# Second projection of an MLP: every third 256-row block of the weight computed by seven half-block products

## The chip, the core and the metric

The kernel runs on one core of a Trainium2 chip. Its time is the device time of one execution in microseconds; the median of three runs is given. Five engines work side by side: TensorE (PE in the profile, with its weight loads apart as PEld) multiplies matrices, VectorE (DVE) and ScalarE (ACT) do elementwise work, GpSimd (POOL) does next to nothing here, and SyncE (SP) issues the transfers from device memory. TensorE writes to eight banks of PSUM, 128 partitions by 512 fp32 columns each; everything else lies in SBUF.

## The reference

A decoder layer on 256 tokens of width 2048: a mixing part with three branches, then the MLP, and a last norm. The change touches the MLP alone, and in it the product with `w_mlp_out`.

```python
h = rmsnorm(x, norm1_g); proj = h @ w_in             # 2048 columns in, three branches, gates
...
x = x + merged @ w_out
h2 = rmsnorm(x, norm2_g)
x = x + jnp.square(jax.nn.relu(h2 @ w_mlp_in)) @ w_mlp_out   # (256,2048)@(2048,8192), then (256,8192)@(8192,2048)
return rmsnorm(x, final_g)
```

All is fp32. To keep its precision, each fp32 operand is split into a high part (rounded to the format fp32r) and a low part (the rest), and a product is three fp32r matmuls: high by high, low by high, high by low.

## The kernel before

**Units.** All weights come in units of 512 KB: 256 rows by 512 columns, held as a tile [128, 2, 512]. `plan` lists the stages of the program, and each stage's units have running numbers, in the order in which TensorE uses them. `dma_to` issues the transfer of a unit on SyncE's queue into a `raw` buffer; there are 4 of them (NRAW), used in turn. `conv_to` makes the two parts: ScalarE copies `raw` to `hi`, which rounds it, and VectorE subtracts, `lo = raw - hi`. `hi` and `lo` have 4 buffers each, in turn. A `raw` buffer is free for the next transfer when the subtraction has read it, a `hi` or `lo` buffer when the last matmul has read it.

**Order.** The order on every engine is that of the program text, and no engine overtakes itself. `begin_unit(u, 3)` stands ahead of the matmuls of unit u: it issues the transfer of unit u+5, then the conversion of unit u+3, then whatever was put off until now by `later` (the reading of finished sums from PSUM, above all). So in VectorE's queue the conversion of unit u+3 stands before the work on sums that comes due at unit u.

**The MLP.** The 8192 hidden columns are done in 4 quarters q. In each, 8 stages `m1` (256 hidden columns each, four units, 16 matmuls a unit, half of them 512 columns wide and half 256) produce the activations, held as `ff` tiles in two parts; then 4 stages `m2` (`run_N`) each multiply them with 512 of the output columns: 8 units, and for each unit 12 matmuls of 512 columns, for two token halves, two 128-row tiles and three products. The sums of a stage lie in one double bank out of two (`two_banks`, pool `ps_mm`, 2 buffers); its end is read one unit later, by two operations of VectorE that add it to the running `x2`, while TensorE works on in the other double bank. Four more single banks (`side`) are not used by these stages. The last stage (`run_last`) orders its matmuls by output, and a norm follows it.

## Time and profile before

| | us |
|---|---|
| median of 3 runs (1542.29 to 1542.65) | 1542.41 |
| the profiled execution, its own time | 1541.8 |
| its span, first to last instruction | 1540.0 |
| TensorE busy | 1529.7 |
| VectorE busy | 1097.5 |
| ScalarE busy | 762.7 |

The profiled execution's time is 1.8 us more than its span, and 0.6 us less than the median. A row of the timeline reads: start in us, duration in us, engine, line, operation, output<-inputs, and in brackets the idle time of the engine before it and what ended it. A row of a group reads: line, engine, operation, names, shapes, count | busy us, mean ns of one | idle time before it and what ended it. A row of the windows reads: stretch in us: its length, then busy time (and count of instructions) of PE, PEld, DVE, ACT and POOL, TensorE's granted clock as a share of full speed, the busy share of the transfer engines, and GB/s. All of VectorE's instructions carry the line of a helper (L86), so they are told apart by names. Matmuls overlap: one of 512 columns is shown as 0.39 us long, and the next starts earlier than it ends.

### The profile page before, as it was taken

To read this page: it belongs to the slowest core of one execution; us is meant where nothing else is said; L and a number is where in the kernel's file an instruction comes from. 1 tells how busy PE (TensorE), PEld (TensorE's weight loads), DVE (VectorE), ACT (ScalarE), POOL (GpSimd) and SP (SyncE) were. 2 spreads that over 40 slices of the span, in tenths; PEclk is the share of its full clock that TensorE was granted. 3 is DMA by queue.
4 is the path that set the end of the run, shared out by engine and by line. 5 is a ranking of instruction groups with operands and counts; after the bars stand their busy time and mean duration, and the time that the engine had idled before them with its cause. 6 is when DMAs were issued, how large, how long until landed. Compare 5 with 4: busy or idle time off the path is not lost.

```text
span 1540.0 us, 20664 instructions
## 1 busy us (share of the span) xinstructions
PE 1529.7 (99%) x7948; PEld 1300.2 (84%) x7948; DVE 1097.5 (71%) x1456; ACT 762.7 (50%) x948; POOL 12.2 (1%) x21
## 2 busy tenths in 40 slices
PE   9999999999999999999999999999999999999997
PEld 9988888888888887898888888888888888888886
DVE  7886978989999999967655665456545655555554
ACT  7446678455555555564454443344433443344442
POOL 0000000000000000000000000000000000000000
PEclk9999999999999999999999999999999999999999
DMA  9654555555555566656666556555555555555653
GB/s 358 200 190 146 188 185 171 185 196 187 189 197 190 193 197 205 191 179 202 209 205 192 191 180 203 192 191 181 198 193 193 181 192 195 195 184 193 217 192 121
DMA packets 85506, 298.17 MB, mean 194 GB/s; under 512 B 9632, under 2 KB 10656, under 8 KB 85408
## 3 DMA queue, kind: packets, MB, share of 16 engines
q1 hardware_dynamic: 79200, 285.25, 55.9%
q10 hardware_dynamic: 6208, 11.61, 2.3%
q8 instruction: 62, 1.02, 0.3%
q14 instruction: 36, 0.29, 0.1%
HBM read 294.73 MB, written 2.10 MB: 193 GB/s over the span
## 4 chain that ended last, share of the span: by engine, by line
PE 96%; DVE 1%; ACT 1%; issue 1%; DMA 0%; POOL 0%; POOLq 0%; DVEq 0%; ACTq 0%
PE mm L288 20%; PE mm L350 20%; PE mm L351 19%; PE mm L353 19%; PE mm L292 10%; PE mm L320 2%; PE mm L319 2%; PE mm L327 1%; PE pb L642 1%; PE py L742 1%; DVE lo L86 0%; PE pwarm L468 0%; DMA raw<-in_w_m 0%; DVE x L86 0%; ACT hi L213 0%
## 5 line engine op out<-in xcount | busy, mean ns | idle before, releaser
L86 DVE TENSOR_TENSOR lo<-raw,hi 128x1024 fp32r<-128x1024 f32 (+1 forms) x537 | 653.7, 1221 | 377.9 <-ACT hi L213 366.1
L213 ACT CAST hi<-raw 128x1024 fp32r<-128x1024 f32 (+1 forms) x537 | 560.6, 1048 | 610.2 <-PE mm L351 377.6
L288 PE MATMUL mm<-xz,hi 128*128 128x512 f32 x1024 | 256.5, 392 | 0.0
L288 PEld LDWEIGHTS mm<-xz,hi 128*128 128x128 f32 x1024 | 184.4, 189 | 33.2
L350 PE MATMUL mm<-hi,xs 128*128 128x512 f32 x512 | 201.4, 393 | 0.0
L351 PE MATMUL mm<-hi,xs 128*128 128x512 f32 x512 | 199.6, 390 | 0.0
L351 PE MATMUL mm<-hi,ff 128*128 128x512 f32 x480 | 186.8, 389 | 0.0
L350 PE MATMUL mm<-hi,ff 128*128 128x512 f32 x480 | 186.8, 389 | 0.0
L292 PEld LDWEIGHTS mm<-xz,lo 128*128 128x128 f32 x1024 | 139.7, 190 | 10.0
L292 PE MATMUL mm<-xz,lo 128*128 128x256 f32 x1024 | 142.8, 282 | 0.0
L353 PE MATMUL mm<-lo,xs 128*128 128x512 f32 x512 | 136.9, 389 | 0.0
L353 PE MATMUL mm<-lo,ff 128*128 128x512 f32 x480 | 128.3, 389 | 0.0
L350 PEld LDWEIGHTS mm<-hi,xs 128*128 128x128 f32 x512 | 96.1, 188 | 23.5 <-issue 4.1
L353 PEld LDWEIGHTS mm<-lo,xs 128*128 128x128 f32 x512 | 96.1, 188 | 20.2
L351 PEld LDWEIGHTS mm<-hi,xs 128*128 128x128 f32 x512 | 96.2, 188 | 19.4
L353 PEld LDWEIGHTS mm<-lo,ff 128*128 128x128 f32 x480 | 90.1, 188 | 18.7
L351 PEld LDWEIGHTS mm<-hi,ff 128*128 128x128 f32 x480 | 90.1, 188 | 18.6
L350 PEld LDWEIGHTS mm<-hi,ff 128*128 128x128 f32 x480 | 90.1, 188 | 18.6
L288 PE MATMUL mm<-xs,hi 128*128 128x512 f32 x384 | 96.9, 394 | 0.0
L288 PEld LDWEIGHTS mm<-xs,hi 128*128 128x128 f32 x384 | 69.1, 189 | 13.6 <-issue 0.7
L86 DVE TENSOR_TENSOR rt<-bu,cs 128x1024 f32<-128x1024 f32 x64 | 76.6, 1220 | 0.3
L292 PEld LDWEIGHTS mm<-xs,lo 128*128 128x128 f32 x384 | 52.4, 190 | 3.8
(247 smaller groups left out, 1619.7 us busy)
## 6 DMA issues: line engine op xcount, KB each, us to landing
raw<-in_w_m SPq DMA_DIRECT2D x256, 512.0 KB, 4.3
raw<-in_w_in SPq DMA_DIRECT2D x143, 512.0 KB, 4.0
raw<-in_w_wide SPq DMA_DIRECT2D x48, 512.0 KB, 3.9
raw<-in_w_br SPq DMA_DIRECT2D x48, 512.0 KB, 4.2
raw<-in_w_out SPq DMA_DIRECT2D x32, 512.0 KB, 3.7
x<-in_x ACTq DMA_DIRECT2D x8, 512.0 KB, 6.1
raw<-in_w_glu SPq DMA_DIRECT2D x8, 512.0 KB, 4.6
gb<-in_b_gate ACTq DMA_DIRECT2D x12, 256.0 KB, 4.3
```

Source lines behind the costliest of these rows:

```text
L86: return fn(*a, **kw)
L213: S.copy(hi[:, k, :], raw[:, k, :])
L288: PE.matmul(pt[:, nb, :], lhsT=hi[:, k, nb * P:(nb + 1) * P], rhs=src.both(4 * i + k), start=4 * i + k == 0, stop=False)
L292: PE.matmul(pt[:, nb, T:], lhsT=lo[:, k, nb * P:(nb + 1) * P], rhs=src.hi(4 * i + k), start=False, stop=4 * i + k == last)
L319: PE.matmul(po, lhsT=wh, rhs=src.hi(kt), start=kt == 0 and nb % 2 == 0, stop=False)
L320: PE.matmul(po, lhsT=wh, rhs=src.lo(kt), start=False, stop=False)
L327: PE.matmul(po, lhsT=lo[:, k, nb * P:(nb + 1) * P], rhs=src.hi(kt), start=False, stop=kt == 2 * nk - 1 and nb % 2 == 1)
L350: PE.matmul(ps[tt], lhsT=xh, rhs=hi[:, k, :], start=kt == 0, stop=False)
L351: PE.matmul(ps[tt], lhsT=xl, rhs=hi[:, k, :], start=False, stop=False)
L353: PE.matmul(ps[tt], lhsT=xh, rhs=lo[:, k, :], start=False, stop=kt == 2 * nk - 1)
L642: PE.matmul(pbs[h][i][:, ri * T:(ri + 1) * T], lhsT=s5bs[h // 4][r, h % 4, ri * P:(ri + 1) * P], rhs=s5x[h // 4][r, h % 4, :], start=True, ...
L742: PE.matmul(py[h][32 * i:32 * i + 32, :T], lhsT=cks[h][:, ri, i, :], rhs=s[i // 2][:, ri, i % 2, :], start=ri == 0, stop=ri == 1, tile_pos ...
```

## The change

The division of the hidden columns and the products of `m2` change; the mixing part, `m1`'s matmuls and the last two stages stay as they are.

- The hidden columns are done in 3 parts of 12, 12 and 8 units (3072, 3072 and 2048 columns). Each `m2` pass of a part now makes 1024 output columns (half h), in all four PSUM banks of `ps_mm`: `top` for the first 128 tokens, `bot` for the others. Only the last two stages of the last part are as before.
- In such a pass, the units k = 0, 3, 6, 9 are done by `run_seven` in another way: a block of 2x2 half blocks (two token halves by two 128-row tiles by two 512-column halves) takes seven products of half blocks in place of eight, in the manner of Strassen and Winograd. Three of its operands on the token side, and three on the weight side, are sums and differences. The token side's four (`form`) are made once in `m1` by `sums`. The weight side's are made from the two transferred tiles in `conv_seven`: there are three conversion units, `a` (as it came), `c` (the difference `d`) and `e` (two more sums, and one half as it came, `b`), out of two transfers. `a`'s raw buffer is read until `e`'s sums, and `c`'s until `e`'s low part is done.
- Four of the seven products go to the four `side` banks, where they are shared by several outputs. They are read one unit after the last seven-product block (`ev_shared`); `top` and `bot` are read right behind their last products (`evac[1]`), at a place in the program that comes after the conversion of the next pass's first units. `m1`'s last group is read at once as well.
- `hi` and `lo` have 5 buffers each, and the pool of activations 32 in place of 34.

```diff
-NACT = 34
+NACT = 32
...
+PARTS = (12, 12, 8)
+FIRST = [sum(PARTS[:q]) for q in range(len(PARTS) + 1)]
+LAST = len(PARTS) - 1
+EVERY = 3
...
-    whi = ctx.enter_context(tc.tile_pool(name="whi", bufs=4))
-    wlo = ctx.enter_context(tc.tile_pool(name="wlo", bufs=4))
+    whi = ctx.enter_context(tc.tile_pool(name="whi", bufs=5))
+    wlo = ctx.enter_context(tc.tile_pool(name="wlo", bufs=5))
...
-    for q in range(4):
-        for i in range(0, 8, 2):
+    for q, nk in enumerate(PARTS):
+        for i in range(0, nk, 2):
+            g = FIRST[q] + i
             if (q, i) == (0, 0):
                 ab = [add_units(w_m1, 0, 0, 3), add_units(w_m1, 1, 0, 3)]
                 for j in range(2):
                     ab[j] += add_units(w_m1, j, 3, 4)
                 plan.append(("m1", (q, i), ab))
             else:
-                plan.append(("m1", (q, i), [add_units(w_m1, 8 * q + i + j, 0, 4) for j in range(2)]))
-        for i in range(4):
-            plan.append(("m2", (q, i), add_units(w_m2, i, 8 * q, 8 * q + 8)))
+                plan.append(("m1", (q, i), [add_units(w_m1, g + j, 0, 4) for j in range(2)]))
+        for h in range(2):
+            if (q, h) == (LAST, 1):
+                for c in (2, 3):
+                    plan.append(("m2", (q, c), add_units(w_m2, c, FIRST[q], FIRST[q + 1])))
+                continue
+            us = []
+            for k in range(nk):
+                ku = FIRST[q] + k
+                if k % EVERY == 0:
+                    n = len(units)
+                    units.extend((w_seven[h, ku // EVERY, 0], w_seven[h, ku // EVERY, 1], None))
+                    seven.update({n: "a", n + 1: "c", n + 2: "e"})
+                    us.append((n, n + 1, n + 2))
+                else:
+                    us.append([add_units(w_m2, 2 * h + c, ku, ku + 1)[0] for c in range(2)])
+            plan.append(("m2s", (q, h), us))
...
+            if units[u] is None:
+                raws.append(None)
+                continue
...
+    def split_unit(u, raw):
+        hi = whi.tile([P, 2, 512], F32R, tag="hi", name=f"hi{u}")
+        lo = wlo.tile([P, 2, 512], F32R, tag="lo", name=f"lo{u}")
+        S.copy(hi, raw)
+        V.tensor_sub(lo, raw, hi.bitcast(F32))
+        return hi, lo
+    def conv_seven(u, raw):
+        if seven[u] == "a":
+            part["a"] = raw
+            loaded[u] = split_unit(u, raw)
+        elif seven[u] == "c":
+            d = part["d"] = s5w.tile([P, 2, 512], F32, tag="T1", name=f"d{u}", bufs=1)
+            part["x"] = raw
+            V.tensor_sub(d, part["a"], raw[:, 0:1, :].to_broadcast([P, 2, 512]))
+            loaded[u] = split_unit(u, d)
+        else:
+            a, d, x = (part.pop(n) for n in "adx")
+            b = s5w.tile([P, 2, 512], F32R, tag="T2", name=f"b{u}", bufs=1)
+            S.copy(b[:, 0, :], x[:, 1, :])
+            V.tensor_sub(b[:, 1, :], x[:, 1, :], b[:, 0, :].bitcast(F32))
+            V.tensor_add(x[:, 0, :], d[:, 1, :], a[:, 0, :])
+            V.tensor_sub(x[:, 1, :], x[:, 1, :], x[:, 0, :])
+            loaded[u] = (*split_unit(u, x), b)
...
-                later(1, lambda pt=pt, evac=evac: evac(pt))
+                if at_once:
+                    evac(pt)
+                else:
+                    later(1, lambda pt=pt, evac=evac: evac(pt))
...
+    def run_seven(us, src, forms, evac):
+        top, bot = two_banks(f"top{us[0][0]}"), two_banks(f"bot{us[0][0]}")
+        bank = {(t, c): p[:, c, :] for t, p in enumerate((top, bot)) for c in range(2)}
+        for n in (1, 5, 7, 6):
+            bank[n] = side(f"p{n}_{us[0][0]}")
...
+        def half(kt, t):
+            return tuple(x[:, t * P:(t + 1) * P] for x in (src.hi(kt), src.lo(kt)))
+        def form(k, f):
+            return tuple(forms[k][:, f, e, :] for e in range(2))
+        def product(b, x, w):
+            mm(b, x[0], w[0])
+            mm(b, x[1], w[0])
+            mm(b, x[0], w[1])
+        def std(u, k, c, t, w):
+            for part in range(2):
+                for e in range(2):
+                    xh, xl = half(2 * k + e, t)
+                    if part == 0:
+                        mm((t, c), xh, w[0][:, e, :])
+                        mm((t, c), xl, w[0][:, e, :])
+                    else:
+                        mm((t, c), xh, w[1][:, e, :])
...
+        shared = max(k for k, u in enumerate(us) if len(u) == 3)
+        for k, u in enumerate(us):
+            if len(u) == 3:
+                a = begin_unit(u[0], 3)
+                product(1, half(2 * k, 0), [w[:, 0, :] for w in a])
+                end_unit()
+                d = begin_unit(u[1], 3)
+                product(5, form(k, 0), [w[:, 0, :] for w in d])
+                product(7, form(k, 2), [w[:, 1, :] for w in d])
+                product((0, 1), form(k, 3), [w[:, 1, :] for w in a])
+                end_unit()
+                hi, lo, b = begin_unit(u[2], 3)
+                product((0, 0), half(2 * k + 1, 0), (b[:, 0, :], b[:, 1, :]))
+                product(6, form(k, 1), (hi[:, 0, :], lo[:, 0, :]))
+                product((1, 0), half(2 * k + 1, 1), (hi[:, 1, :], lo[:, 1, :]))
+                if k == shared:
+                    later(1, lambda: evac[0](bank))
+                end_unit()
+            elif k < len(us) - 1:
+                for c in range(2):
+                    w = begin_unit(u[c], 3)
+                    for t in range(NT):
+                        std(u[c], k, c, t, w)
+                    end_unit()
+            else:
+                w0 = begin_unit(u[0], 3)
+                std(u[0], k, 0, 0, w0)
+                end_unit()
+                w1 = begin_unit(u[1], 3)
+                std(u[1], k, 1, 0, w1)
+                evac[1](0, top)
+                std(u[0], k, 0, 1, w0)
+                std(u[1], k, 1, 1, w1)
+                evac[1](1, bot)
+                end_unit()
...
+            def sums():
+                f = s5w.tile([P, 4, P], F32, tag="gb", name=f"sums{q}_{i}", bufs=1)
+                V.scalar_tensor_tensor(out=f[:, 0, :], in0=t[:, 0, P:], scalar=-1.0, in1=t[:, 1, P:],
+                                       op0=ALU.mult, op1=ALU.subtract)
+                V.scalar_tensor_tensor(out=f[:, 1, :], in0=f[:, 0, :], scalar=-1.0, in1=t[:, 0, :P],
+                                       op0=ALU.mult, op1=ALU.subtract)
+                V.tensor_sub(f[:, 2, :], t[:, 0, :P], t[:, 0, P:])
+                V.tensor_sub(f[:, 3, :], t[:, 1, :P], f[:, 1, :])
+                fs = forms[q][i] = a4([P, 4, 2, P], F32R, f"form{q}_{i}")
+                S.copy(fs[:, :, 0, :], f)
+                V.tensor_sub(fs[:, :, 1, :], f, fs[:, :, 0, :].bitcast(F32))
...
+                run_W([g], xs2, at_once=i0 + j == PARTS[q] - 1)
...
+    def do_m2s(q, h, us):
+        if q == LAST:
+            load_fg()
+        r = [a4([P, 2, 512], F32, f"m2r{q}{h}{t}") for t in range(NT)]
+        def ev_shared(bank):
+            p1, p12 = r[0][:, 0, :], r[0][:, 1, :]
+            p21, p22 = r[1][:, 0, :], r[1][:, 1, :]
+            S.copy(p1, bank[1])
+            S.copy(p12, bank[5])
+            V.tensor_add(p21, bank[6], p1)
+            V.tensor_add(p12, p12, p21)
+            V.tensor_add(p22, bank[7], p12)
+            V.tensor_add(p21, bank[7], p21)
+        def ev(t, ps):
+            V.tensor_add(r[t], ps, r[t])
+            for c in range(2):
+                later(1 + t, lambda c=c: add_m2(q, 2 * h + c, t, 0, 512, r[t][:, c, :]))
+        run_seven(us, ffs[q], forms[q], (ev_shared, ev))
...
+    b = a["w_m2"].reshape(2, 2, -1, P, 2, 512)[:, :, ::EVERY]
+    a["w_seven"] = np.stack([np.stack([b[:, r, :, :, 0], b[:, 1 - r, :, :, 1]], axis=3) for r in range(2)],
+                            axis=2)
```

**VectorE where one pass of the second projection ends and the next begins.** Names: `lo` is the low part of a weight unit, `mm` a double bank with finished sums, `x` the running output. Before, first part, from output columns 0 to 511 on to the next 512:

```order
L86 TENSOR_TENSOR lo_8405<-raw_8366,hi_8404 128x1024
L86 TENSOR_TENSOR lo_8423<-raw_8384,hi_8422 128x1024
L86 TENSOR_TENSOR lo_8441<-raw_8402,hi_8440 128x1024
L86 TENSOR_TENSOR lo_8460<-raw_8420,hi_8459 128x1024
L86 SCALAR_TENSOR_TENSOR x_0_6813<-mm_8304,rsq,x_0_6813 128x512 x2
L86 TENSOR_TENSOR lo_8480<-raw_8438,hi_8479 128x1024
L86 TENSOR_TENSOR lo_8498<-raw_8457,hi_8497 128x1024
L86 TENSOR_TENSOR lo_8516<-raw_8477,hi_8515 128x1024
```

The two sums are taken up in the middle of a row of conversions of plain units. In the change, from columns 0 to 1023 on to the next 1024; `m2r` is the tile into which the shared products and the sums are added, `p` a single bank, `d`, `b` and the second use of `raw` the weight sums of the next pass's first block:

```order
L91 TENSOR_TENSOR m2r_8728<-m2r_8728,m2r_8729 128x512
L91 TENSOR_TENSOR m2r_8729<-p_328_8734,m2r_8728 128x512
L91 TENSOR_TENSOR m2r_8729<-p_328_8734,m2r_8729 128x512
L91 TENSOR_TENSOR lo_9152<-raw_9112,hi_9151 128x1024
L91 TENSOR_TENSOR d_9169<-raw_9112,raw_9127 128x1024
L91 TENSOR_TENSOR lo_9172<-d_9169,hi_9171 128x1024
L91 TENSOR_TENSOR b_9183<-raw_9127,b_9183 128x512
L91 TENSOR_TENSOR raw_9127<-d_9169,raw_9112 128x512
L91 TENSOR_TENSOR raw_9127<-raw_9127 128x512
L91 TENSOR_TENSOR lo_9189<-raw_9127,hi_9188 128x1024
L91 TENSOR_TENSOR m2r_8728<-top_8730,m2r_8728 128x1024
L91 TENSOR_TENSOR m2r_8729<-bot_8731,m2r_8729 128x1024
```

The two operations on finished sums stood between conversions of plain units and nothing waited for them but the sums after next; now the two that read `top` and `bot` stand behind the three conversions a, c and e of the next pass.

**TensorE at the same place.** In the change, the end of the first pass (plain units of block 11) and the beginning of the second (products of block 0):

```order
L436 MATMUL bot_8731<-lo_9115,ff_11_8743 128x512 x2
L436 MATMUL bot_8731<-hi_9129,ff_11_8743 128x512 x4
L436 MATMUL bot_8731<-lo_9130,ff_11_8743 128x512 x2
L436 MATMUL p_356_9216<-hi_9151,ff_0_7732 128x512 x2
L436 MATMUL p_356_9216<-lo_9152,ff_0_7732 128x512
L436 MATMUL p_356_9217<-hi_9171,form_0_7765 128x512 x2
L436 MATMUL p_356_9217<-lo_9172,form_0_7765 128x512
L436 MATMUL p_356_9218<-hi_9171,form_0_7765 128x512 x2
L436 MATMUL p_356_9218<-lo_9172,form_0_7765 128x512
L436 MATMUL top_9214<-hi_9151,form_0_7765 128x512 x2
L436 MATMUL top_9214<-lo_9152,form_0_7765 128x512
```

Before, the next stage's first matmuls went to the other double bank. Now the third group of the new pass is written to `top` (`top_9214`), the same two banks as the `top_8730` just finished. The other passes end alike: after the second pass `m1`'s first group, and after the last part's pass the first plain stage, write to `top`'s banks at once.

**VectorE over one group of blocks, 3 to 5.** In the change (7 units for three blocks; the four rows at the end are the plain units), where before stood one `lo` a unit:

```order
L91 TENSOR_TENSOR lo_8798<-raw_8764,hi_8797 128x1024
L91 TENSOR_TENSOR d_8815<-raw_8764,raw_8779 128x1024
L91 TENSOR_TENSOR lo_8818<-d_8815,hi_8817 128x1024
L91 TENSOR_TENSOR b_8835<-raw_8779,b_8835 128x512
L91 TENSOR_TENSOR raw_8779<-d_8815,raw_8764 128x512
L91 TENSOR_TENSOR raw_8779<-raw_8779 128x512
L91 TENSOR_TENSOR lo_8841<-raw_8779,hi_8840 128x1024
L91 TENSOR_TENSOR lo_8859<-raw_8813,hi_8858 128x1024
L91 TENSOR_TENSOR lo_8868<-raw_8833,hi_8867 128x1024
L91 TENSOR_TENSOR lo_8883<-raw_8856,hi_8882 128x1024
L91 TENSOR_TENSOR lo_8898<-raw_8865,hi_8897 128x1024
```

The seven units of such a group have eleven operations of VectorE, where the six units of three plain blocks had six `lo`; each row here waits for a copy by ScalarE, except `d` and the two sums on `raw`.

## Rows read from the trace of the kernel before

**Rows 1.** The page: span, busy time by engine, the chain that ended last.

```profile
span 1540.0 us, 20664 instructions
...
PE 1529.7 (99%) x7948; PEld 1300.2 (84%) x7948; DVE 1097.5 (71%) x1456; ACT 762.7 (50%) x948; POOL 12.2 (1%) x21
...
PE 96%; DVE 1%; ACT 1%; issue 1%; DMA 0%; POOL 0%; POOLq 0%; DVEq 0%; ACTq 0%
```

**Rows 2.** Timeline, TensorE: one unit of the second projection and the next's start.

```profile
1101.89 0.39 PE L350 MATMUL mm<-hi,ff 128*128 128x512 f32 x1
...
1103.70 1.07 PE L353 MATMUL mm<-lo,ff 128*128 128x512 f32 x4
1104.61 0.39 PE L350 MATMUL mm<-hi,ff 128*128 128x512 f32 x1
```

**Rows 3.** Windows of one quarter's first projection, then of its second.

```profile
855.00:914.00 59.00, 59.00 (x341) 51.96 (x340) 36.35 (x37) 27.41 (x33) 0.00 (x0) 1.00 0.58 192
914.00:1004.00 90.00, 90.00 (x403) 74.72 (x403) 47.08 (x44) 35.89 (x36) 0.00 (x0) 1.00 0.58 193
```

**Rows 4.** Timeline of the second projection, ScalarE, then VectorE.

```profile
1112.06 1.05 ACT L213 CAST hi<-raw 128x1024 fp32r<-128x1024 f32 x1 [1.67 <-PE mm L351]
...
1113.14 1.23 DVE L86 TENSOR_TENSOR lo<-raw,hi 128x1024 fp32r<-128x1024 f32 x1 [1.49 <-ACT hi L213]
1114.28 1.40 DVE L86 SCALAR_TENSOR_TENSOR x<-mm,rsq,x 128x512 f32<-128x512 f32 x2
```

**Rows 5.** Groups by form, whole span, VectorE and ScalarE.

```profile
L86 DVE TENSOR_TENSOR lo<-raw,hi 128x1024 fp32r<-128x1024 f32 x535 | 652.3, 1223 | 377.3 <-ACT hi L213 365.5 <-PE mt L408 6.0 <-PE zt L408 4.5
L86 DVE TENSOR_TENSOR bu<-rt,rt 128x512 f32<-128x512 f32 x64 | 42.4, 693 | 0.4
L86 DVE TENSOR_TENSOR relu<-mm,relu 128x512 f32<-128x512 f32 x32 | 21.9, 684 | 0.0
L86 DVE SCALAR_TENSOR_TENSOR ck<-cu,cu 128x128 f32<-128x128 f32 x8 | 2.3, 285 | 0.0
...
L213 ACT CAST hi<-raw 128x1024 fp32r<-128x1024 f32 x535 | 559.3, 1050 | 609.7 <-PE mm L351 377.6 <-PE mm L288 119.9 <-issue 71.5
L399 ACT CAST ff<-relu 128x512 fp32r<-128x512 f32 x32 | 19.8, 619 | 60.9 <-DVE relu L86 60.9
L301 ACT COPY relu<-mm 128x512 f32<-128x512 f32 x32 | 18.7, 583 | 0.0
```

**Rows 6.** What SyncE's queue waited for, us in total, times, longest us.

```profile
SPq L194 <- DVE lo L86: 1231.2, 504, 7.8
```

**Rows 7.** Transfers of raw from issue to landing: 1098 to 1130, then 10 to 19 us.

```profile
DMA to landing us min/median/max: 3.7/4.3/4.5
...
DMA to landing us min/median/max: 6.1/6.5/7.5
```

**Rows 8.** The chain near the end, and the timeline of ScalarE there.

```profile
1510.77 4.32 DMA raw<-in_w_m
...
1515.10 1.05 ACT L213 CAST hi<-raw 128x1024 fp32r<-128x1024 f32 x1 [1.56 <-DMA raw<-in_w_m]
```

**Rows 9.** Windows of the end: TensorE's last matmuls, then none.

```profile
1531.00:1532.00 1.00, 0.69 (x6) 0.49 (x5) 0.27 (x1) 0.00 (x0) 0.00 (x0) 1.00 0.00 0
1532.00:1536.00 4.00, 0.00 (x0) 0.00 (x0) 2.47 (x7) 0.51 (x2) 0.55 (x1) 1.00 0.26 98
1536.00:1537.00 1.00, 0.00 (x0) 0.00 (x0) 0.00 (x0) 0.00 (x0) 0.00 (x0) 0.71 1.07 318
```

**Rows 10.** Timeline, TensorE: 256-column matmuls near the start, and a little later.

```profile
6.54 0.41 PE L320 MATMUL mm<-xs,hi 128*128 128x256 f32 x1
6.75 0.41 PE L319 MATMUL mm<-xs,hi 128*128 128x256 f32 x1
...
8.07 0.28 PE L320 MATMUL mm<-xs,hi 128*128 128x256 f32 x1
8.19 0.28 PE L319 MATMUL mm<-xs,hi 128*128 128x256 f32 x1
```

More of the change, by code (lines that the diff above doesn't have):

```diff
@@ L141, in side @@
         return ps_sd.tile([P, 512], F32, tag="sd", name=name)
-    units = []
+    units, seven = [], {}
     def add_units(src, g, k0, k1):
@@ L204, in conv_to @@
             raws[u] = None
+            if u in seven:
+                conv_seven(u, raw)
+                nconv[0] += 1
+                continue
             if u >= len(units) - 4:
@@ L358, in run_N, with mm @@
             end_unit()
+    def run_seven(us, src, forms, evac):
[3 more added lines that the diff above has]
+            bank[n] = side(f"p{n}_{us[0][0]}")
+        triples = sum(len(u) == 3 for u in us)
+        left = {b: 6 * (len(us) - triples) for b in bank if b not in (1, 5, 6, 7)}
+        for b in (1, 5, 6, 7, (0, 0), (0, 1), (1, 0)):
+            left[b] = left.get(b, 0) + 3 * triples
+        begun = set()
+        def mm(b, x, w):
+            left[b] -= 1
+            PE.matmul(bank[b], lhsT=x, rhs=w, start=b not in begun, stop=left[b] == 0)
+            begun.add(b)
+        def half(kt, t):
[50 more added lines that the diff above has]
+                end_unit()
+        assert not any(left.values())
@@ L1089, in square @@
                 split2(ffs[q], i, t)
+                if i % EVERY == 0:
+                    later(1, sums)
+            def sums():
[9 more added lines that the diff above has]
+                V.tensor_sub(fs[:, :, 1, :], f, fs[:, :, 0, :].bitcast(F32))
             later(1, square)
@@ L1096, in do_m1 @@
         else:
[L1097 to L1123 removed]
+            for j, g in enumerate(groups):
+                run_W([g], xs2, at_once=i0 + j == PARTS[q] - 1)
@@ new lines, in load_fg, with add_m2 @@
+    def load_fg():
+        for j in range(2):
+            f = a4([P, 2, 512], F32, f"fg{j}")
+            S.dma_start(f, final_g[j * 1024:(j + 1) * 1024].rearrange("(a c) -> a c", a=2)
+                        .partition_broadcast(P))
+            fg.extend((f[:, 0, :], f[:, 1, :]))
+        fg.append(a4([P, NT, 512], F32, "last"))
+    def add_m2(q, c, tt, c0, c1, ps):
+        v = x2[c][:, tt, c0:c1]
+        V.scalar_tensor_tensor(out=v, in0=ps, scalar=st2["rsq"][:, tt:tt + 1], in1=v,
+                               op0=ALU.mult, op1=ALU.add)
+        if q == LAST:
+            n = c + (c0 > 0)
+            sumsq(v, ss3[:, tt, n:n + 1], ps)
+            V.tensor_mul(v if c < 3 else fg[4][:, tt, c0:c1], v, fg[c][:, c0:c1])
+            if c == 3 and c1 == 512:
+                finish(tt)
```

37 lines of the change are left out of this document (12 added, 25 removed).

## The prediction, made before the changed kernel ran

> **What bounds the kernel now.** Read the page first: TensorE is busy 99% of the span, and 96% of the chain that ended last is matmuls [rows 1]. In the stages that change, the windows say the same: TensorE is busy in all of both stretches, VectorE in 36.35 of 59.00 and 47.08 of 90.00 us, ScalarE in less [rows 3]. So a matmul taken away is time saved, as long as VectorE and ScalarE deliver. How they deliver today is in the timeline: in the second projection a copy of ScalarE waits 1.67 us for a matmul to free its buffer, and VectorE's subtraction 1.49 us for that copy [rows 4]. Both wait for TensorE, once in each unit's 2.72 us. SyncE's queue in its turn waits for VectorE: 504 transfers wait for `lo` [rows 6]. The four raw buffers are thus full when the copies want them. That is the cover on which the change draws.
>
> **What is saved.** The matmuls of a plain unit begin at 1101.89 and those of the next at 1104.61: 2.72 us for 12, 0.2267 us each [rows 2]. A block by the new way has 21 matmuls of 512 columns in place of 24. There are 4 such blocks in each of two passes of two parts, and 3 in one pass of the last: 19 blocks, 57 matmuls, **12.9 us**. What the Trainium skill says of the price differs: "TensorE: Matmul & The Clock Gate", section "Back-to-back issue gap", gives about 131 ns as the sustained spacing of 512-column matmuls; by it the saving would be 7.5 us. The row decides, and the sum goes by the row.
>
> **What VectorE and ScalarE get.** Durations: 1024 elements 1.23 us on VectorE, but the next independent instruction starts 1.14 after (1113.14 to 1114.28); the copy 1.05, and 0.03 from its end (1113.11) to VectorE's start [rows 4]. 512 elements take 0.69, from PSUM 0.68, and about 0.08 less to an independent successor, as above: 0.61; ScalarE's copies of 512 take 0.62 and 0.58; 128 elements 0.285 [rows 5]. A conversion on its own is 0.03 + 1.05 + 0.03 + 1.23 = 2.34 us. The operations on broadcast and in-place operands do not occur in the trace in that form; they can cost nothing less than the rows of their size show, and I see no reason for more.
>
> A group (one new block, two plain) takes TensorE 69 x 0.2267 = 15.64 us. VectorE's work in it: 4 plain `lo` and `lo`(a) 5 x 1.14, `d` 1.15, `lo`(c) 1.14, three halves 1.95, `lo`(e) 1.23: 11.2 us. By busy time that fits. But two things make it a chain. `lo`(c) waits for `d` and its copy, `lo`(e) for the sums and their copy, while nothing else may pass in VectorE's queue. And the raw buffers turn: `c`'s buffer is held until `lo`(e) is done, and the fourth plain unit of the group is the next to be loaded into it. A transfer takes 3.7 to 4.5 us, median 4.3 [rows 7]; the chain near the end shows the wait whole, 4.32 us from 1510.77, and the copy at 1515.10, 4.33 after [rows 8]. So, counted from the end of `lo`(e) of one group:
>
> - 4.33 until the fourth plain unit's data are there, 1.05 + 0.03 + 1.23 for its parts: 6.65
> - `lo`(a) of the next block 1.14, `d` 1.15: 8.95
> - `lo`(c) 2.34: 11.3; half `b` 0.61, two sums 0.61 and 0.72: 13.2; `lo`(e) 2.34: **15.6**.
>
> The loop takes 15.6 us, TensorE's group 15.64. So it holds, with nothing to spare; the conversions neither gain on TensorE nor lose.
>
> **How far ahead they are.** `lo`(e) is wanted 3.85 us after a pass's first matmul (3 of a, 9 of c, 5 of e). Its conversion waits for the sums of `m1`'s last group but one, which end 11.1 us before the pass (4 units of 2.77: eight matmuls of 512 columns at 0.2267 and eight of 256 at 0.12 [rows 2, 10]). From there: 0.2 + 0.53 (copy) + 1.05 + 0.03 + 1.15 (`lo`(a)) + 2.1 (square, its copy, its low part) + 1.15 (`d`) + 2.34 + 1.95 + 2.34 = 12.8, done 1.7 after the start, 2.2 ahead. In the first group the last `m1` sums stand between: relu 0.6, `lo` 1.14, square 0.72, copy 0.65, the second plain unit's copy and `lo` 2.2, so 5.3; only then is the raw buffer of the next c free: 4.33, `d` 1.2, 2.34, 1.95, 2.34: 17.5 us against 15.64. That takes 1.9, and some 0.3 us of lead are left at each pass's end. In the last part `sums` of unit 6 (4 x 0.285, a copy and a low part, 2.5 us in all) fall into the same queue ahead of `lo`(e): the lead becomes 2.1 us of waiting. **+2.1.**
>
> **Where a pass ends.** Here the change adds a wait, and this decides. Behind the last new block stand in VectorE's queue, counted as above from `lo`(e): the four plain units (6.65, by the raw buffer), the four adds of the shared banks 0.61 + 0.72 + 0.72 + 0.61 (9.3), then `lo`(a) 1.14, `d` 1.15, c 2.34, halves 1.95, e 2.34 of the next pass (18.2), and only then the add that frees `top`, 1.2: 19.4. With 0.3 of lead, `lo`(e) was done 0.85 after e's first matmul, so `top` is free 20.3 us after it. TensorE wants to write `top` again after 9 matmuls of e, 48 of the four units, 3 of a and 6 of c: 66 x 0.2267 = 14.96. It stands for **5.3 us**, at two places. What is late next: e's products and all behind them by as much; the conversions do not depend on it and come ahead, which the adds to `x2` (4 x 0.61) then use up.
>
> Into `m1` there are three plain units in place of a, c, e: 9.3 + 3 x 1.14 + 1.2 + 0.85 = 14.8 against 57 matmuls, 12.9: **1.9 us**, twice. In the last part only one plain block follows the last new one: VectorE has two plain units and one of the next stage, then the fourth by the raw buffer (6.65), the adds (9.3), one unit 1.14, the add 1.2: 11.6 + 0.85 = 12.5, and TensorE comes after 33 matmuls, 7.5: **5.0 us**.
>
> **What costs nothing.** The `form` operations (11 times 2.5 us) lie in `m1`, where VectorE idles 22.6 of 59 us [rows 3]; without that cover they would be 27 us. The last groups' sums read at once only have to be out before `bot` is written, 18 matmuls later. Transfers are as many as before. The fifth `hi` and `lo` buffers and the 32 tiles leave the order ahead of the MLP as it was; TensorE's share of the chain there leaves them nothing to win.
>
> **Sum.** On the profiled execution's own 1541.8 us (span 1540.0): -12.9 + 2.1 + 2 x 5.3 + 2 x 1.9 + 5.0 = +8.6, 1550.4. The median lies 0.6 above that execution: **1551.0 us**. The uncertain term is the transfer's wait, once in each loop and each ending. With 3.7 us the loop takes 15.0, three loops and the ending gain 2.4: the waits become 2.9 twice, 0 twice, 3.2 and 1.5, in sum 10.5, and the time 1540.0. At 4.7 the loop is 0.4 too long, 14 loops: 1557. The far row, 6.1 to 7.5 us [rows 7], is from a stretch where other large transfers run at once; I take 4.3, which the second projection itself shows.
>
> **Rivals.**
> - *The conversions keep far ahead* (faster). If the raw buffers don't bind, VectorE's loop is 13.4 us (11.2 of work and two copies of 1.1 that it waits for), and they run ahead as far as five buffers let them. Then the adds wait for TensorE itself: its product for the last shared bank ends 1.5 after e's start, copies 1.1, adds 2.66, then 8.9 to the end of `lo`(e) and 1.2: 15.4 against 14.96. Waits of 0.4 twice and 0.1: 1542.4 - 12.9 + 0.9 = 1530.4. For it: VectorE's busy time. Against: 504 transfers that wait for `lo`. It begins to hold when a transfer takes under some 3 us: four waits, in three loops and the ending, then give back the 5.3.
> - *The waits just eat the saving* (no change): transfers of 3.6 to 4.0 us; 1539.5 to 1545.
> - *TensorE's clock falls in the waits* (slower still). At the kernel's end TensorE has its last matmul at 1531.69; the granted clock is 1.00 until 1536 and 0.71 in the next microsecond [rows 9], which with levels of 2.4 and 1.2 GHz is a fall some 4.7 us after. Three waits here are 4.5 to 5.3 us. Matmuls near the kernel's start stand 0.21 us apart, later 0.12 [rows 10]; at most the first 7 us are like that, half of it lost. So 0 to 3.4 us a fall, I take 2.5: 1551 + 7.5 = 1558.5. The same page of the Trainium skill, section "Why this matters for your kernels", says so too: gaps between bursts return the clock to its lower level. The rows bear it out for the end alone.
>
> **Chances.** Forecast 0.50 (own range 1545.5 to 1556); clock falls 0.12 (1555 to 1562); no change 0.17; far ahead or nearly so 0.21 (1530 to 1539). About 0.2% (3.1 us) is what a measurement can tell from no change, 1539.3 to 1545.5; faster 0.21, same 0.17, slower 0.62. The range reaches from 1537 (half of the fast case) to 1559.
>
> **What would show it.** Right: TensorE idle for 4.5 to 5.5 us in the c unit of each second pass, released by VectorE's add that reads `top`; 1.5 to 2 us at `m1`'s start after a part; about 5 before the first plain stage of the last part; ScalarE's copies waiting for transfers in the passes; 57 matmuls fewer. Wrong: copies that still wait for TensorE, then the transfers don't bind and the fast case holds; or a granted clock below 1.00 inside the span. A transfer time off by 0.3 us moves the result by some 5 us, and that is what would make the prediction wrong.

## The result and the profile after

The changed kernel takes 1558.19 us, median of 4 runs (1557.39 to 1559.23), beside 1542.43 for the kernel before. The ratio is 1.0102, interval 1.0085 to 1.012: slower by 1.0%, 15.8 us. The forecast was 1551.0, range 1537 to 1559, with 1545.5 to 1556 as the forecast's own narrower range.

The page of the changed kernel, against [rows 1]:

```profile
span 1555.8 us, 20817 instructions
...
PE 1528.9 (98%) x7891; PEld 1293.0 (83%) x7891; DVE 1207.8 (78%) x1628; ACT 790.6 (51%) x1007; POOL 12.3 (1%) x21
...
PE 88%; DVE 5%; ACT 3%; issue 2%; DMA 2%; SPq 0%; ACTq 0%; POOLq 0%; DVEq 0%; POOL 0%
```

TensorE has 57 matmuls fewer, and its share of the chain has gone from 96% to 88%. In the stages that changed it now waited for these (us in total, times, longest):

```profile
PE top L436 <- DVE m2r L91: 8.6, 2, 4.3
PE mm L410 <- DVE m2r L91: 4.7, 1, 4.7
PE p L436 <- DVE lo L91: 1.7, 4, 0.5
...
PE p L436 <- ACT hi L251: 1.0, 2, 0.5
...
PE mm L345 <- DVE m2r L91: 0.4, 1, 0.4
```

The first two rows are the three long waits: between the passes of parts 0 and 1, and ahead of the first plain stage of the last part. VectorE's timeline around the first of them shows the whole chain, from the low part of the last new block's e at 1009.33 to the adds that read `top` and `bot`:

```profile
1009.33 4.63 DVE L91 TENSOR_TENSOR lo<-raw,hi 128x1024 fp32r<-128x1024 f32 x4 [1.19 <-ACT hi L251]
1016.45 1.22 DVE L91 TENSOR_TENSOR lo<-raw,hi 128x1024 fp32r<-128x1024 f32 x1 [2.50 <-ACT hi L241]
1017.60 0.68 DVE L91 TENSOR_TENSOR m2r<-p,m2r 128x512 f32<-128x512 f32 x1
...
1020.32 1.21 DVE L91 TENSOR_TENSOR lo<-raw,hi 128x1024 fp32r<-128x1024 f32 x1
1021.45 1.22 DVE L91 TENSOR_TENSOR d<-raw,raw 128x1024 f32<-128x1024 f32 x1
1023.86 1.23 DVE L91 TENSOR_TENSOR lo<-d,hi 128x1024 fp32r<-128x1024 f32 x1 [1.19 <-ACT hi L251]
...
1028.20 1.23 DVE L91 TENSOR_TENSOR lo<-raw,hi 128x1024 fp32r<-128x1024 f32 x1 [1.19 <-ACT hi L251]
1029.34 1.22 DVE L91 TENSOR_TENSOR m2r<-top,m2r 128x1024 f32<-128x1024 f32 x1
```

From the end of lo(e) (1009.33 + 1.23) to the end of the add (1030.56) it is 20.0 us; the forecast had 19.4. VectorE's wait of 2.50 us is for the copy of the fourth plain unit. ScalarE's timeline says that this copy waited for a transfer, and SyncE's that the transfer was issued at 1010.58, when lo(e), the last reader of the raw buffer that c held, had just ended (1010.56):

```profile
1015.37 1.05 ACT L241 CAST hi<-raw 128x1024 fp32r<-128x1024 f32 x1 [2.86 <-DMA raw<-in_w_m]
```

```profile
1010.58 0.33 SPq L218 DMA_DIRECT2D raw<-in_w_m  x1
```

TensorE's timeline shows what the add released:

```profile
1025.94 0.39 PE L436 MATMUL p<-lo,form 128*128 128x512 f32 x1
1030.61 1.22 PE L436 MATMUL top<-hi,form 128*128 128x512 f32 x2 [4.28 <-DVE m2r L91]
...
1032.06 1.48 PE L436 MATMUL top<-b,ff 128*128 128x512 f32 x3
1033.34 1.05 PE L436 MATMUL p<-hi,form 128*128 128x512 f32 x2
```

In windows of the same place the third number from the end (PEclk) is the granted clock:

```profile
1026.00:1028.00 2.00, 0.33 (x2) 0.00 (x0) 0.98 (x2) 0.88 (x1) 0.00 (x0) 0.91 0.33 104
1028.00:1030.00 2.00, 0.00 (x0) 0.00 (x0) 1.80 (x2) 2.00 (x3) 0.00 (x0) 0.50 0.42 162
1030.00:1032.00 2.00, 1.39 (x3) 1.16 (x4) 2.00 (x3) 1.10 (x2) 0.00 (x0) 0.50 0.78 233
1032.00:1034.00 2.00, 2.00 (x6) 1.55 (x5) 2.00 (x3) 1.05 (x1) 0.00 (x0) 0.50 0.31 55
1034.00:1036.00 2.00, 2.00 (x9) 1.62 (x9) 2.00 (x4) 0.00 (x1) 0.00 (x0) 0.88 0.62 236
```

The clock falls inside the wait, before 1028, and is back at 1.00 only after 1034. In each of the three long waits it is at 0.50 (1.2 GHz) for 6.83 us, of which 3.9, 5.9 and 4.6 us lie behind the wait. The matmuls there stand 0.427 us apart (three of them from 1032.06 to 1033.34) where 0.2267 is usual; summed up that costs 1.9, 2.9 and 2.2 us, 7.0 in all.

### The profile page after: what moved, and what is told of

It reads as the page before. It is cut to its first block, busy times and chain, and to the rows that moved or that the text cites. A ratio compares the mean times of both kernels' runs of the same rounds, so it can differ in the third digit from the quotient of the medians.

```text
span 1555.8 us, 20817 instructions
## 1 busy us (share of the span) xinstructions
PE 1528.9 (98%) x7891; PEld 1293.0 (83%) x7891; DVE 1207.8 (78%) x1628; ACT 790.6 (51%) x1007; POOL 12.3 (1%) x21
## 4 chain that ended last, share of the span: by engine, by line
PE 88%; DVE 5%; ACT 3%; issue 2%; DMA 2%; SPq 0%; ACTq 0%; POOLq 0%; DVEq 0%; POOL 0%
PE mm L345 19%; PE mm L410 12%; PE mm L411 12%; PE mm L413 12%; PE mm L349 10%; PE top L436 7%; PE bot L436 6%; PE p L436 3%; DVE lo L91 2%; PE mm L379 1%; PE mm L387 1%; PE mm L380 1%; ACT hi L251 1%; DMA raw<-in_w_m 1%; ACT hi L241 1%
## 5 line engine op out<-in xcount | busy, mean ns | idle before, releaser
L91 DVE TENSOR_TENSOR lo<-raw,hi 128x1024 fp32r<-128x1024 f32 (+1 forms) x537 | 644.5, 1218 | 166.3 <-ACT hi L241 132.4
L241 ACT CAST hi<-raw 128x1024 fp32r<-128x1024 f32 (+1 forms) x499 | 514.3, 1048 | 255.7 <-PE mm L411 112.8
L411 PEld LDWEIGHTS mm<-hi,xs 128*128 128x128 f32 x512 | 96.2, 188 | 19.4
L436 PE MATMUL bot<-hi,ff 128*128 128x512 f32 x334 | 91.5, 391 | 0.1
L436 PE MATMUL top<-hi,ff 128*128 128x512 f32 x296 | 79.5, 390 | 0.0
L251 ACT CAST hi<-raw 128x1024 fp32r<-128x1024 f32 x38 | 40.0, 1051 | 68.8 <-DVE raw L91 46.7
L436 PEld LDWEIGHTS bot<-hi,ff 128*128 128x128 f32 x334 | 63.0, 189 | 13.5 <-DVE relu L91 0.4
L436 PEld LDWEIGHTS top<-hi,ff 128*128 128x128 f32 x296 | 55.9, 189 | 11.9
L91 DVE TENSOR_TENSOR relu<-mm,relu 128x512 f32<-128x512 f32 x32 | 22.1, 690 | 41.8 <-ACT relu L361 41.8
```

What stands on the lines that cost most here:

```text
L91: return fn(*a, **kw)
L241: S.copy(hi[:, k, :], raw[:, k, :])
L251: S.copy(hi, raw)
L411: PE.matmul(ps[tt], lhsT=xl, rhs=hi[:, k, :], start=False, stop=False)
L436: PE.matmul(bank[b], lhsT=x, rhs=w, start=b not in begun, stop=left[b] == 0)
```

## The experiments

All start from the changed kernel; the kernel before took 1541.8 to 1542.3 us (medians) beside them.

**Plain blocks in the new passes.** No block is done by the new way.

```diff
-                if k % EVERY == 0:
+                if k < 0:
...
-            V.tensor_add(r[t], ps, r[t])
+            V.tensor_copy(r[t], ps)
```

> All blocks of the second projection by the plain way (24 matmuls each, no form operations), in the changed kernel's passes, parts and buffers. Queue theory (the add that frees the first pair of banks stands behind the next pass's conversions, and these wait for a raw buffer that a new block holds): without new blocks no buffer is held, VectorE has three low parts ahead of the add and is done with them early, so the waits where a pass ends fall from about 5 us to under 0.5, the clock stays at 1.00, and the 57 matmuls come back: 1558.2 - 20.5 - 7.1 + 12.9 = 1543.5 us (1541 to 1545), as before the change. Rival (a pass that fills all eight banks of PSUM has to wait at its end whatever its blocks are): waits of 4 to 5 us stay at two to three ends, with the clock's price: 1553 to 1571 us.

Measured 1543.83 us, ratio 1.001 (1.0001 to 1.002). No row of TensorE's waits names `m2r`. So the passes, which here fill the four banks of `ps_mm` and leave the `side` banks unused, and the buffers cost some 1.5 us (0.2 to 3.1 by the interval); the rest belongs to the new blocks and the banks that they share.

**The buffer of c freed early.** The sums go into d's tile.

```diff
-            V.tensor_add(x[:, 0, :], d[:, 1, :], a[:, 0, :])
-            V.tensor_sub(x[:, 1, :], x[:, 1, :], x[:, 0, :])
-            loaded[u] = (*split_unit(u, x), b)
+            V.tensor_add(d[:, 1, :], d[:, 1, :], a[:, 0, :])
+            V.tensor_sub(d[:, 0, :], x[:, 1, :], d[:, 1, :])
+            loaded[u] = (*split_unit(u, d), b)
...
```

The two products of e swap the halves that they read, to match.

> The two sums of a new block's third unit are written into d's tile, which nothing reads any more, in place of the raw buffer of c; that buffer is free some 2.3 us earlier (before the third conversion instead of behind it). No instruction more or less. Queue theory with the held buffer: the loop of conversions falls from 15.6 to 13.3 us against TensorE's 15.64, the conversions gain on TensorE, and at a pass's end the transfer's wait begins 2.3 us earlier: waits between passes 1 to 3 us in place of 5.7, 2.6 at the last part's end in place of 4.9; the clock falls in one of them or in none. 1558.2 - 2 x 3.5 - 2.3 - 4 to 7 = 1542 us (1537 to 1547). Rival (VectorE's and ScalarE's work for a new block is too long in itself, the buffer doesn't matter): waits as before, 1556 to 1560 us.

Measured 1545.16 us, ratio 1.0016 (1.0006 to 1.0025): 13 us back from an edit that adds nothing and takes nothing away. VectorE's two lo(e) of the third and fourth block of a pass show the length of the loop; between them stands lo(a):

```profile
993.28 1.23 DVE L91 TENSOR_TENSOR lo<-d,hi 128x1024 fp32r<-128x1024 f32 x1 [1.19 <-ACT hi L251]
...
1000.47 1.22 DVE L91 TENSOR_TENSOR lo<-raw,hi 128x1024 fp32r<-128x1024 f32 x1 [1.22 <-ACT hi L251]
...
1008.38 1.23 DVE L91 TENSOR_TENSOR lo<-d,hi 128x1024 fp32r<-128x1024 f32 x1 [1.19 <-ACT hi L251]
```

The loop is 15.10 us; in the changed kernel it is 16.11:

```profile
993.22 4.63 DVE L91 TENSOR_TENSOR lo<-raw,hi 128x1024 fp32r<-128x1024 f32 x4 [1.20 <-ACT hi L251]
...
1001.43 1.23 DVE L91 TENSOR_TENSOR lo<-raw,hi 128x1024 fp32r<-128x1024 f32 x1 [0.74 <-ACT hi L251]
```

The next lo(e) there is the row at 1009.33 above. The loop with the buffer freed was to be 13.3. What the sum did not have is the wait ahead of lo(a), 1.22 us: a's copy waits for a transfer that is issued only at 995.68, when the low part of the first plain unit has freed its raw buffer. The idle 1.19 us ahead of d's and e's low parts, which the sum had, are still there. In the profiled execution, the slowest of the ten (1547.27), three waits of 1.8 to 3.0 us are left, each with a fall of the clock.

**The add that reads `top` ahead of c and e.**

```diff
-                w0 = begin_unit(u[0], 3)
+                w0 = begin_unit(u[0], 2)
...
-                w1 = begin_unit(u[1], 3)
+                w1 = begin_unit(u[1], 1)
                 std(u[1], k, 1, 0, w1)
                 evac[1](0, top)
+                conv_to(u[1] + 2)
```

> In the last pair of a pass the conversions of the next pass's c and e (and of plain units in their place) are issued behind the add that frees the first pair of banks, not ahead of it. Queue theory: that add is done about 8 us earlier, but d, c and e are late by its 1.1 us, and TensorE then waits for e's low part instead: between passes some 1.1 us for d and 1.8 us for e in place of 5.7 in one piece; at the last part's end 1.1 us less. The clock stays up between the passes. 1558.2 - 2 x 2.5 - 1.1 - 4.8 = 1547 us (1544 to 1552). Rival (the place in the queue doesn't matter, since the conversions set the pace anyway): the waits move to e's products with their whole length, 1555 to 1560 us.

Measured 1549.6 us, ratio 1.0048 (1.0033 to 1.0063). TensorE's timeline between the passes has, in place of one wait, these:

```profile
1024.48 0.73 PE L436 MATMUL p<-hi,form 128*128 128x512 f32 x2 [1.37 <-ACT hi L251]
1025.74 0.50 PE L436 MATMUL p<-lo,form 128*128 128x512 f32 x1 [0.53 <-DVE lo L91]
...
1029.96 0.74 PE L436 MATMUL p<-hi,form 128*128 128x512 f32 x2 [1.61 <-ACT hi L251]
1031.22 0.50 PE L436 MATMUL p<-lo,form 128*128 128x512 f32 x1 [0.52 <-DVE lo L91]
```

The wait goes from `top` to d's and e's products, 4.0 us in four pieces where 2.9 was expected, and the clock, which was to stay up between the passes, fell there once, to 0.50 for 3.41 us. At the last part's end 0.67 and 0.87 us are left of 4.74, a larger gain than the 1.1 expected. The time is inside the expected range. The place in the queue makes the wait one piece; that the conversions are late stays.

**TensorE kept at work in the three waits.**

```diff
...
+                if keep and k == 0:
+                    for _ in range(17):
+                        PE.matmul(bank[6], lhsT=half(0, 0)[0], rhs=a[0][:, 0, :], start=True, stop=True)
                 product((0, 1), form(k, 3), [w[:, 1, :] for w in a])
...
```

Ahead of the first plain stage of the last part it is 19 matmuls, in the same way.

> TensorE gets 17 matmuls more in each of the two waits between passes and 19 ahead of the first plain stage of the last part, all into a bank of PSUM that is not in use and whose result nothing reads. If the waits themselves let the clock fall: the added matmuls (3.9 and 4.3 us) lie inside waits of 4.3 to 4.7 us, the clock stays at 1.00, and the 7.1 us of slow matmuls are given back: 1551 us (1550 to 1553); this also gives the waits without the clock, to set against the forecast's sum. Rival (the clock falls there for another reason, or the time is lost elsewhere): the low stretches stay, and the time is 1557 to 1561 us.

Measured 1555.66 us, ratio 1.0087 (1.0072 to 1.0102). The granted clock stays at 1.00, in windows across the first of the three places too:

```profile
1028.00:1030.00 2.00, 2.00 (x11) 1.64 (x10) 1.26 (x2) 2.00 (x3) 0.00 (x0) 1.00 0.66 242
1030.00:1032.00 2.00, 1.61 (x8) 1.01 (x7) 2.00 (x2) 1.67 (x2) 0.00 (x0) 1.00 0.48 166
```

So the waits had let it fall. But of the 7.0 us only 2.5 come back, less than the 5 to 8 expected. The list of TensorE's waits says where most of the rest is:

```profile
PE mm L345 <- DVE m2r L91: 2.9, 2, 1.5
PE p L440 <- DVE lo L91: 2.6, 5, 0.5
```

The two waits into `m1` are now 1.5 us each, where the changed kernel had 0.4 in all. The slow matmuls had given the late conversions time. What the clock costs by itself and what it costs in the end are not the same number; the expectation had taken them for one.

**Six raw buffers, four `hi` and `lo`.**

```diff
-NRAW = 4
+NRAW = 6
...
-    whi = ctx.enter_context(tc.tile_pool(name="whi", bufs=5))
-    wlo = ctx.enter_context(tc.tile_pool(name="wlo", bufs=5))
+    whi = ctx.enter_context(tc.tile_pool(name="whi", bufs=4))
+    wlo = ctx.enter_context(tc.tile_pool(name="wlo", bufs=4))
```

> The changed kernel with six raw buffers in place of four, paid with four hi and four lo buffers in place of five each; the order of the work is the same. Queue theory with the held buffer: the same as the run that frees the buffer of c early, by another edit. No copy waits 2.5 us for a transfer in the passes any more (31 and 12 times in the changed kernel), the conversions gain on TensorE, and the waits where a pass ends go from 5.7 to between 1 and 3 us: 1538 to 1548 us; more, 1550, if four hi and lo buffers keep the conversions from running ahead. Rival (the earlier gain came from something else in that edit than the buffer): 1555 to 1560 us.

Measured 1546.89 us, ratio 1.0036 (1.0023 to 1.0049): the second way of taking away the wait for the buffer gives much the same. The copies' waits for a transfer in the passes are gone from ScalarE's list; five waits of TensorE of 1.8 to 2.2 us stand at the passes' ends, two of them into `m1` (in the profiled execution, the slowest of the five, 1550.11).

**The form operations of unit 6 later.**

```diff
-                    later(1, sums)
+                    later(6 if (q, i) == (LAST, 6) else 1, sums)
```

> Of the changed kernel one thing alone is moved: the form operations of unit 6 of the last part (four of 128 elements, a copy and a low part) are issued behind the conversions of the pass's first new block, in place of ahead of them. The forecast's term for the start of the last part (2.1 us; the waits there were 3.1 us in the changed kernel's trace) says: waits there fall to under 1 us, nothing else changes, 1555.5 us (1554.5 to 1556.5). Rival (that start is late because of the first group's relu and square, not of the sums): 1557.5 to 1558.5 us.

Measured 1558.66 us, ratio 1.0112 (1.0096 to 1.0129): nothing gained. The first new block's lo(e) comes 2.1 us earlier (1451.82 for 1453.90), the second's 0.5 later (1472.81 for 1472.27), since the sums now stand ahead of that one. TensorE's small waits in that pass add up to as much as before: what the sums take from VectorE they take at either place.

**Both edits at once**, the buffer freed early and `top` read first.

> Both edits that were tried singly: the buffer of c is free early, and the add that frees the first banks stands ahead of the next pass's c and e. Queue theory: the first edit takes the loop, the second the place in the queue, and they add up. Of the 18.5 us that the first alone still lost after 700 us (waits of 3.2, 2.0 and 2.9 us, their slow matmuls, and 2.5 at the last part's start) the three waits fall to under 1 us each, and the clock stays up or falls once: 1545.2 - 6 - 3 to 5 = 1535 us (1533 to 1539), faster than the kernel before. Rival (the conversions of the next block take the place of the add and TensorE waits for them as long): 1543 to 1547 us.

Measured 1545.63 us, ratio 1.0025 (1.0015 to 1.0034). A miss: no better than the first edit alone. The rival named there holds. TensorE waits in the new blocks again (`p` for ScalarE's copies 4.4 us, for `lo` 3.7), so the conversion of a new block itself was too long.

**New blocks at the second, fifth, ... place.**

```diff
-                if k % EVERY == 0:
+                if k % EVERY == 1 and k < nk - 1:
...
```

> The new blocks stand at the second, fifth, eighth (and eleventh) place of a pass in place of the first, fourth and so on; each pass begins with a plain block; 18 new blocks (54 matmuls saved, 12.2 us) in place of 19. In VectorE's queue stand behind the last new block's lo(e): four low parts with one transfer's wait (6.65 us), the shared adds (2.66), the low part of the next a (1.14), the add that frees the banks (1.2), in sum 11.65, against 33 matmuls (7.5 us). Queue theory: a wait of 5.3 us less the lead of the conversions, which is larger than before, since each pass has two plain units of time first (2 to 5 us); so 0.3 to 3 us at four places, none at the last part's end: 1542.4 - 12.2 + 2 to 12 + clock 0 to 8 = 1541 us (1532 to 1550). Rival (what a pass begins with is all that matters, since a plain block needs no long conversions): no waits, 1530 to 1532 us. Other rival (the new blocks' work is too long wherever they stand): 1555 to 1560 us.

Measured 1569.55 us, ratio 1.0181 (1.0165 to 1.0196), slower than any and far outside the 1532 to 1550 expected. The chain's 11.65 us against 33 matmuls are there in full, at all four places and not at the last part's end:

```profile
PE mm L345 <- DVE m2r L91: 9.0, 2, 4.6
PE top L436 <- DVE m2r L91: 8.9, 2, 4.6
```

What failed is the lead of 2 to 5 us that I gave it. There was none: already in the first new block of a pass TensorE waits 0.78 us for d's copy and 0.53 for its low part (at 969.17 and 970.43 in part 0).

**The operations of a new block in another order.** After these runs VectorE's idle 1.19 us, which stands twice in each new block above, ahead of d's low part and of e's, was left as the suspect.

```diff
         elif seven[u] == "c":
...
+            x = part["x"] = raw
+            a, b = part.pop("a"), s5w.tile([P, 2, 512], F32R, tag="T2", name=f"b{u}", bufs=1)
+            part["b"] = b
             S.copy(b[:, 0, :], x[:, 1, :])
+            d = s5w.tile([P, 2, 512], F32, tag="T1", name=f"d{u}", bufs=1)
+            V.tensor_sub(d, a, x[:, 0:1, :].to_broadcast([P, 2, 512]))
...
+            S.copy(hi, d)
             V.tensor_sub(b[:, 1, :], x[:, 1, :], b[:, 0, :].bitcast(F32))
             V.tensor_add(x[:, 0, :], d[:, 1, :], a[:, 0, :])
             V.tensor_sub(x[:, 1, :], x[:, 1, :], x[:, 0, :])
-            loaded[u] = (*split_unit(u, x), b)
+            V.tensor_sub(lo, d, hi.bitcast(F32))
+            loaded[u] = (hi, lo)
+        else:
+            loaded[u] = (*split_unit(u, part.pop("x")), part.pop("b"))
```

> The changed kernel with the operations of one new block in another order, none more or less: ScalarE copies b ahead of d, VectorE forms d, b's low part and the two sums, and only then d's low part and e's. In the traces so far VectorE stands 1.19 us twice in each new block, once for the copy of d and once for that of e; in this order other work lies there. Theory now (VectorE's queue has its waits and its work in each group, and more work at a pass's end, than TensorE's 15.64 us allow): the chain from the end of one lo(e) to the next is 6.65 (transfer, copy, low part) + 1.14 + 1.15 + 1.95 + 1.14 + 1.23 = 13.3 us in place of 15.6, c's buffer is held 2.3 us less too, the conversions gain 2 us in each group, and where a pass ends 17.0 us less the lead stand against 14.96: waits of 0 to 2 us in place of 5.7, 2.5 at most at the last part's end, the clock falls at most once. 1542.4 - 12.9 + 2 to 10 = 1536 us (1531 to 1541), faster than before. Rival (the buffer and the queue's place were all that mattered, and those are hardly changed): waits of 3 to 4 us between passes, 1545 to 1552 us.

Measured 1530.76 us, ratio 0.9928 (0.9913 to 0.9942): 11.2 us faster than the kernel before, with the instructions of the changed one, and 0.2 below the 1531 to 1541 expected. VectorE's timeline has one block without a gap:

```profile
995.87 1.23 DVE L91 TENSOR_TENSOR lo<-raw,hi 128x1024 fp32r<-128x1024 f32 x1 [0.40 <-ACT hi L251]
997.01 1.22 DVE L91 TENSOR_TENSOR d<-raw,raw 128x1024 f32<-128x1024 f32 x1
998.15 0.69 DVE L91 TENSOR_TENSOR b<-raw,b 128x512 fp32r<-128x512 f32 x1
998.75 0.68 DVE L91 TENSOR_TENSOR raw<-d,raw 128x512 f32<-128x512 f32 x1
999.47 0.69 DVE L91 TENSOR_TENSOR raw<-raw 128x512 f32<-128x512 f32 x1
1000.08 1.22 DVE L91 TENSOR_TENSOR lo<-d,hi 128x1024 fp32r<-128x1024 f32 x1
1001.36 1.23 DVE L91 TENSOR_TENSOR lo<-raw,hi 128x1024 fp32r<-128x1024 f32 x1
```

From lo(a) to the end of lo(e) it takes 6.7 us; in the changed kernel 9.1 (1001.43 to 1010.56). The plain copies behind it, in ScalarE's timeline, wait for TensorE again, as they did in [rows 4]:

```profile
1002.76 1.05 ACT L241 CAST hi<-raw 128x1024 fp32r<-128x1024 f32 x1 [1.43 <-PE bot L440]
1005.48 1.05 ACT L241 CAST hi<-raw 128x1024 fp32r<-128x1024 f32 x1 [1.67 <-PE bot L440]
```

One wait of 0.9 us, at the last part's end, is left of all, and the clock does not fall before the kernel's end.

**The same, with `top` read ahead of e** (the second unit of the last pair begins with a lead of 2, and the next unit is converted behind the add).

> The order of the run before in this list, and besides the add that frees the first banks ahead of e's last two conversions (behind those of c). If the conversions have a lead of more than 2 us at a pass's end, this is worth nothing between passes (0 to 1 us) and helps at the last part's end by one low part (1.1 us): 1530 to 1536 us, and within 1.5 us of the run without it. If they have no lead, it takes up to 1.2 us of each of the two waits between passes: 2 to 4 us faster than without it.

Measured 1529.92 us, ratio 0.9922 (0.9905 to 0.9939), the best of all and 0.8 below the run before, as expected where there is a lead. Against the plain blocks in the same passes (1543.83) it is 13.9 us faster.

**The new order with six raw and four `hi` and `lo` buffers.**

> The same order of operations with six raw buffers and four hi and lo buffers. If transfers still set the pace with the new order, the waits that are left go with them: 1530 to 1533 us. If VectorE's work sets it (13.3 us less the transfer's 2.1 of waiting is 11.2 us in a group, 2.7 more where a pass ends), there is nothing left to gain, and the four hi and lo buffers, which hold the conversions to TensorE's pace, cost up to 2 us at each pass's end: 1533 to 1541 us.

Measured 1538.05 us, ratio 0.9975 (0.9965 to 0.9984): 7.3 us more than with four raw and five `hi` and `lo`. ScalarE's copy, VectorE's add and TensorE at the end of part 0:

```profile
1083.00 1.05 ACT L241 CAST hi<-raw 128x1024 fp32r<-128x1024 f32 x1 [3.02 <-PE bot L440]
```

```profile
1085.23 1.22 DVE L91 TENSOR_TENSOR m2r<-top,m2r 128x1024 f32<-128x1024 f32 x1
```

```profile
1086.59 1.84 PE L349 MATMUL mm<-xz,hi 128*128 128x512 f32 x4 [1.82 <-DVE m2r L91]
```

The fourth unit ahead needs a `hi` buffer that the pass's last matmuls still read; the add stands behind it in VectorE's queue. By this trace the fifth buffers are a part of the change that pays.

## Why the prediction came out as it did

The sign, the places and the wait behind VectorE's queue were right; a term left at nothing, the clock, made the size. The time lies 0.8 us inside the stated range and 2.2 outside the forecast's own narrower one, and the forecast's own sign of being wrong came: a granted clock below 1.00 inside the span. In the transfers, which it named as what would make it wrong, the errors went both ways: the fourth plain unit's low part starts 4.9 to 5.0 us behind lo(e) within the first pass and 5.9 behind it at the pass's end, for 5.4 in the sum.

- *Saved 12.9 us by 57 matmuls.* Held. With the waits gone the chip gives 11.2 and 12.0 us against the kernel before, 13.1 and 13.9 against plain blocks in the same passes. By the spacing that the Trainium skill gives, "TensorE: Matmul & The Clock Gate", section "Back-to-back issue gap", an estimate of 7.5 us would have come: the trace disagrees, 0.2267 us a matmul, and so does this time.
- *A first pass's lo(e) done 1.7 us after the start.* 1.70: it ends at 961.07, the pass begins at 959.37.
- *The loop, 15.6 against 15.64.* 16.1 to 16.2 measured. Within the pass the fourth plain unit's low part came 0.4 us sooner than in the sum, but then VectorE stood 0.7 to 0.9 us for the next a's copy, which the sum did not have. So the loop lost half a microsecond a group instead of just holding.
- *Second passes, 5.3 us each.* 4.28 and 4.27 on `top`, and ahead of that d's copy or low part: 0.50 and 0.53 in part 0, 0.52 in part 1. With the matmuls' restarts, 6.0 and 5.4 between their starts. Held.
- *Into `m1`, 1.9 us each.* 0.4 in all with the slow clock, 1.5 each with the clock kept up: near the term, but in the changed kernel itself it was paid as slow matmuls.
- *The last part's end, 5.0 us.* 4.74. Held.
- *The last part's start, 2.1 us, for the sums ahead of lo(e).* 3.1 us of small waits in that pass. That the sums stand ahead of the first lo(e) is not the reason: moved behind it, they cost as much.
- *The clock stays up.* This step failed. The forecast took 4.7 us from the kernel's end [rows 9] as what a wait must last, and gave the fall a chance of 0.12. It fell in all three long waits. That rival had the time, 1558.5, and its price of 2.5 us a fall is near the 7.0 for three. The Trainium skill, "TensorE: Matmul & The Clock Gate", section "Why this matters for your kernels", had warned that gaps between bursts return the clock to its lower level; the trace agrees, with 0.50 behind waits of 4.27 to 4.74 us.

The forecast's waits sum to 21.5 us. Measured from matmul to matmul, less 0.23 (1030.61 - 1025.94 - 0.23 = 4.44 for the wait of 4.28), they are 6.0, 5.4, 0.6, 4.9, 3.1 in the last part's pass, and 0.5 elsewhere: 20.5. With 7.0 for the clock, less 12.9 saved, that is 14.6 of the span's 15.8; the run with plain blocks alone has some 1.5 for the passes themselves. That the two sums of waits agree is in part luck: the waits into `m1` are 0.6 here for 3.8, since the slow matmuls cover them, and the second passes, the last part's start and small waits elsewhere make up for two thirds of that.

The rival *conversions keep far ahead*, 1530.4 us, was rejected for a transfer's wait. The new order shows it possible (1530.8) with transfers of much the same length (medians 4.2 and 4.0 us, where the changed kernel has 4.2 and 4.7), not under the 3 us that the rival was to need. The forecast had the 1.1 us copies in its loop, as 2.34 for each conversion on its own, without asking whether other work could stand there. How much of the 27 us the filled gaps give and how much the earlier release of c's buffer, which comes with them, was not separated further; freeing the buffer alone gave 13.

## What to carry to other kernels

Where a queue that works in order waits for a helper in the middle of a chain, look first for independent work that can stand there: here that was worth 27 us, together with the earlier release of a buffer that came with it, and with no instruction more or less. An engine that is busy 78% of the span can still set the pace in the stage that counts; compare its chain, waits included, with the other engine's group, and do not count on a loop that comes out equal: 15.6 by the sum was 16.1. A wait of TensorE costs its own length and can then cost matmuls at half the clock (1.9 to 2.9 us a fall here); those in turn hide other lateness, so the two cannot be added up term by term.
